# A two-layer decoder trunk on one core: the down products' add to the residual moves from VectorE into PSUM, with copies by ScalarE

## The chip, the core and the metric

The kernel runs on one core of a Trainium2 chip. The core has a matrix engine (TensorE, PE in the profile, with its weight loads as PEld), a vector engine (VectorE, DVE), a scalar engine (ScalarE, ACT), a general engine (GpSimd, POOL) and a queue that issues transfers (SyncE, SP). Each engine works through its own instructions in the order in which they stand; semaphores make one wait for another. Matrix products go to PSUM, eight banks of 128 x 512 fp32 numbers; everything else lies in SBUF. The metric is the device time of one execution in microseconds. Between two versions, a difference under 0.2% is about what a measurement can't tell from none.

## The reference

The trunk has two layers on 256 tokens of width 2048. Each layer has a token mixer with a cross-attention and then a SwiGLU feed-forward block; the residual `h` runs through all of it. The change touches the second line below, in both layers.

```
h = h + jnp.concatenate([y, xa], axis=-1) @ w_out[layer]
hn = _rmsnorm(h, norm_ffn[layer])
gate, up = jnp.split(hn @ w_gate_up[layer], 2, axis=-1)   # 2048 -> 2 x 5632
h = h + (jax.nn.silu(gate) * up) @ w_down[layer]          # 5632 -> 2048
```

## The kernel before

**Precision by parts.** Weights and left factors are fp32. Each is taken apart into a high part (a cast to fp32r) and a low part (the rest), and a product is three matmuls: high x high, high x low of the weights, low of the factor x high. So every weight tile costs a DMA into a tile `raw` (4 buffers), a cast on ACT (L207) and a subtraction on DVE (L208), both written into a tile `parts` (6 buffers). The cast's result is enough for a product's first and third matmul; the second needs the subtraction. This pair is called a split below.

**The feed-forward stage** (`ffn`) goes over 11 blocks of 512 columns (b = 0 to 10). `up_block(b)` makes gate and up in one: it goes over eight pairs of weight rows with a scheme of seven products (`project_halves`), whose sums `ps[1]` to `ps[7]` (p1 to p7 below) fill seven PSUM banks. A pair of kind S splits its weights in four pieces, a to d: a and b as loaded, c and d after DVE has combined the raw tile with itself (L350 to L352). Blocks 3 to 10 have the pairs S S O S S O S S, so they end on two S. Then ACT copies p1 out to `e` (L830), DVE adds the other sums in a row (L833, first `s<-p2`, then `e<-p6`, `s<-p7`, `e<-p5` and so on), and ACT's Silu (L835) and a product on DVE (L836) end the block. Its result is transposed on PE (L160) and split into left factors (L148, L149).

**The down products.** The 5632 rows of `w_down` are cut into six parts (`PARTS`), one block or two each. `down(i, n)` multiplies part i into the n-th 512 columns of the residual with `project`: two PSUM banks, one for each half of the tokens, and per two rows of weights one split, named 192_0, 192_2, 193_0 and so on after the raw tile. Then `add_h` adds each bank to the residual with a DVE instruction (L414). After each up block from b = 1 on, two down products are done; the last part's four stand at the end, and its adds are followed by what the next layer or the output needs.

**Order.** The code is written in program order, and a scheduler that lists the instructions ahead of the run places each on its engine's queue: by priority in program order, but as soon as its inputs and a free buffer or bank are there by the scheduler's own reckoning. Banks are given out from a pool of eight as they come free. So an edit can move instructions that it does not name. Small pieces of other work (`later`, `step`) are given out between matmuls.

Names: `f_p` are the sums of an up block, `fd` those of a down product, `h` the residual, `tp` the transposes; in this stage layer 0 has the raw tiles 84 to 215, layer 1 those from 288 to 419. The functions that the change touches, with their lines:

Of the kernel before, what the change touches and what calls it, by code (L numbers as in the profile page):

```python
# [17 lines left out]
P = 128  # L18
T = 256
NT = T // P  # L20
# [15 lines left out]
def trunk_kernel(ctx: ExitStack, tc: tile.TileContext, x, mem, norm_mix, norm_ffn, norm_mem,  # L36
                 norm_final, hgrn_w_in, hgrn_lb_logits, hgrn_onorm, gla_w_in, gla_w_gk,
                 gla_b_gk, gla_onorm, w_mem_kv, w_out, w_gate_up, w_down, c_ident, c_mask, out):
    nc = tc.nc
# [15 lines left out]
    ident = const.tile([P, P], F32, name="ident")  # L55
# [15 lines left out]
    h = const.tile([P, NT, D], F32, name="h")  # L71
# [83 lines left out]
    def transposes(srcs, name):  # L155

        ps = aux_ps(name)
        for k, src in enumerate(srcs):
            for t in range(NT):
                nc.tensor.transpose(out=ps[:, k * T + t * P:k * T + (t + 1) * P], in_=src(t), identity=ident)  # L160
        return ps

    def make_quad(quad, src, gains, same=False):

# [36 lines left out]
    def split(src, name, by=2):  # L201

        n, m = src.shape[1:]
        both = wts.tile([P, 2, 2, 512], F32R, tag="parts", name=f"parts{name}", bufs=6)
        for k in range(0, n, by):
            j = min(k + by, n)
            nc.scalar.copy(out=both[:, 0, k:j, 0:m], in_=src[:, k:j, :])  # L207
            nc.vector.tensor_tensor(out=both[:, 1, k:j, 0:m], in0=src[:, k:j, :],  # L208
                                    in1=both[:, 0, k:j, 0:m].bitcast(F32), op=ALU.subtract)
        return [(both[:, 0, k, 0:m], both[:, 1, k, 0:m]) for k in range(n)]  # L210

    def weights(w, k0, nk, c0, n):
        i, raw = new_raw()
        m = 1 if i == 0 else nk
        for j in range(0, nk, m):
            nc.sync.dma_start(out=raw[:, j:j + m, 0:n],
                              in_=w[(k0 + j) * P:(k0 + j + m) * P, c0:c0 + n].rearrange("(k p) c -> p k c", p=P))
        return [p for k in range(0, nk, 2) for p in split(raw[:, k:k + 2, 0:n], f"{i}_{k}", 1 if i == 0 else 2)]

    def project(quads, order, w, c0, n, name, parts=None, prep=None, by_tile=None):  # L220

        parts = parts or [(0, n)]
        ps = [[mm_ps(f"{name}_{i}_{t}") for t in range(NT)] for i in range(len(parts))]
        if by_tile is None:
            groups = [([qi], range(NT)) for qi in range(len(order))]
        else:
            groups = [(range(len(order)), [t]) for t in range(NT)]  # L230
        got = {}
        for qis, ts in groups:
            for qi in qis:
                q = order[qi]
                if prep:
                    prep(q)
                if qi not in got:
                    got[qi] = weights(w, 4 * q, 4, c0, n)
                for k, (hi, lo) in enumerate(got[qi]):
                    if k == 2 or (k == 0 and qi > 0):  # L240
                        step()
                    first = qi == 0 and k == 0
                    last = qi == len(order) - 1 and k == 3
                    for t in ts:
                        xh = quads[q].h[:, k, t * P:(t + 1) * P]
                        xl = quads[q].l[:, k, t * P:(t + 1) * P]
                        for i, (o, m) in enumerate(parts):
                            acc = ps[i][t][:, 0:m]
                            nc.tensor.matmul(acc, xh, hi[:, o:o + m], start=first, stop=False)  # L249
                            nc.tensor.matmul(acc, xh, lo[:, o:o + m], start=False, stop=False)  # L250
                            nc.tensor.matmul(acc, xl, hi[:, o:o + m], start=False, stop=last)  # L251
            if by_tile is not None:
                by_tile(ts[0], ps[0][ts[0]])
        return ps if len(parts) > 1 else ps[0]
# [66 lines left out]
    def project_halves(forms, kinds, w, c0, c1, name):  # L321


        left = {b: sum(TIMES[kind][b - 1] for kind in kinds) for b in range(1, 8)}
        ps = {}

        def product(b, left_factor, right):
            first = b not in ps
            if first:
                ps[b] = bank(f"{name}p{b}")  # L330
            left[b] -= 1
            (xh, xl), (hi, lo) = left_factor, right
            nc.tensor.matmul(ps[b], xh, hi, start=first, stop=False)  # L333
            nc.tensor.matmul(ps[b], xh, lo, start=False, stop=False)  # L334
            nc.tensor.matmul(ps[b], xl, hi, start=False, stop=left[b] == 0)  # L335

        for p, kind in enumerate(kinds):
            i, raw = new_raw()

            for j, c in ((slice(0, 4, 3), c0), (slice(1, 3), c1)):  # L340
                nc.sync.dma_start(out=raw[:, j, :],
                                  in_=w[2 * p * P:(2 * p + 2) * P, c:c + 512].rearrange("(k p) c -> p k c", p=P))
            x = forms[p].get
            last = p == len(PAIRS) - 1
            if kind == "S":
                tt = nc.vector.tensor_tensor
                b00, = split(raw[:, 0:1, :], f"{i}a")
                b11, b10 = split(raw[:, 2:4, :], f"{i}b")

                tt(out=raw[:, 0:2, :], in0=raw[:, 0:4:2, :], in1=raw[:, 1:2, :].broadcast_to([P, 2, 512]), op=ALU.subtract)  # L350
                tt(out=raw[:, 2, :], in0=raw[:, 2, :], in1=raw[:, 0, :], op=ALU.add)  # L351
                tt(out=raw[:, 3, :], in0=raw[:, 3, :], in1=raw[:, 2, :], op=ALU.subtract)  # L352
                t5, t7 = split(raw[:, 0:2, :], f"{i}c")
                t6, t4 = split(raw[:, 2:4, :], f"{i}d")
                todo = {1: ("x00", b00), 2: ("x01", b10), 3: ("z", b11), 4: ("x11", t4), 5: ("s", t5), 6: ("u", t6),
                        7: ("d0", t7)}
                for b in (1, 2, 6, 7, 5, 4, 3) if last else (1, 3, 2, 5, 7, 6, 4):
                    product(b, x(todo[b][0]), todo[b][1])
            else:
                b00, b01 = split(raw[:, 0:2, :], f"{i}a")  # L360
                b11, b10 = split(raw[:, 2:4, :], f"{i}b")
                todo = [[(2, "x00", b00), (5, "x10", b01), (4, "x10", b00), (3, "d0", b01)]]
                if kind == "O":
                    todo.append([(2, "x01", b10), (5, "x11", b11), (4, "x11", b10), (3, "d1", b11)])
                else:
                    nc.vector.tensor_tensor(out=raw[:, 3, :], in0=raw[:, 3, :], in1=raw[:, 2, :], op=ALU.subtract)
                    e1, = split(raw[:, 3:4, :], f"{i}c")
                    todo.append([(2, "x01", b10), (3, "x01", b11), (7, "x11", b11), (4, "x11", e1)])
                todo = [m for ms in zip(*todo) for m in ms] if last else todo[0] + todo[1]
                for b, f, right in todo:  # L370
                    product(b, x(f), right)
            step()
        return ps
# [14 lines left out]
    def h_forms(forms, n, gain, ss, name):  # L388

        for t in range(NT):  # L390
            square_sum(h[:, t, n * 512:(n + 1) * 512], ss[:, t, n:n + 1], f"{name}{n}{t}")

        def turn(p):
            forms[p] = Forms(p, f"{name}{p}")
            ps = aux_ps(f"tp_{name}{p}")
            for i, (t, k) in enumerate(((1, 0), (0, 0), (0, 1), (1, 1))):
                c = (2 * p + k) * P
                nc.tensor.transpose(out=ps[:, i * P:(i + 1) * P], in_=h[:, t, c:c + P], identity=ident)
            forms[p].put(ps, [gain[:, 2 * p + k:2 * p + k + 1] for k in range(2)])

        later(lambda: turn(2 * n), lambda: turn(2 * n + 1))
# [9 lines left out]
    def add_h(ps, c0, n):  # L411
        for t in range(NT):
            hs = h[:, t, c0:c0 + n]
            nc.vector.tensor_tensor(out=hs, in0=ps[t][:, 0:n], in1=hs, op=ALU.add)  # L414
# [402 lines left out]
    PARTS = ((0,), (1, 2), (3, 4), (5, 6), (7, 8), (9, 10))  # L817
# [4 lines left out]
    def ffn(l, forms, r, after, tail=None):  # L822
# [21 lines left out]
        def down(i, n):  # L844
            end = i == len(PARTS) - 1
            if end and n == NQ - 1 and tail:
                flush()
                project(sq, PARTS[i], w_down[l], 512 * n, 512, f"fd{l}_{i}_{n}", by_tile=tail)
                return
            ps = project(sq, PARTS[i], w_down[l], 512 * n, 512, f"fd{l}_{i}_{n}")  # L850
            add_h(ps, 512 * n, 512)
            if end:
                after(n)

        todo = []
        for b in range(DFF // 512):
# [101 lines left out]
```

## Time and profile before

| | us |
|---|---|
| median of three runs | 2323.41 |
| lowest and highest | 2322.97, 2323.65 |
| the profiled execution | 2322.12 |
| its span (first to last instruction) | 2320.3 |
| feed-forward of layer 0, its first and last matmul start | 540.9, 1244.0 |
| feed-forward of layer 1, its first and last matmul start | 1610.0, 2310.6 |

PE's granted clock is 0.998 of full speed over the span. The page of the profile gives busy time as a share of the span for each engine; such a share is a mean over stages. In this kernel the mixers (the time ahead of 540.9 and from 1244.0 to 1610.0 us) and the feed-forward stages differ: DVE is busy in 5 to 6 tenths of most slices in the first and in 9 tenths of most in the second. Rows of single instructions give the start from the span's beginning, the duration, the engine, the line, the operation, what it writes and reads, shapes, and in brackets how long the engine had been idle before it and what ended that. Matmuls overlap: a row's duration is longer than the time to the next start.

### The profile page before, as it was taken

What the parts mean: (1) busy time and instruction counts of PE and PEld (TensorE: products, weight loads), DVE (VectorE), ACT (ScalarE), POOL (GpSimd) and SP (SyncE); (2) the same over time, 40 slices, a digit from 0 to 9 for tenths busy, and PEclk for the clock granted to TensorE, in tenths of its full rate; (3) what the DMA queues carried; (4) which work ended last, traced back from release to release, by engine and by line L of the source; (5) the groups of instructions that cost most, each with busy time, mean ns of one, the idle gap of its engine ahead of it and who ended that gap; (6) DMA issues with size and microseconds to landing.
All of it is one profiled execution on the core that took longest, in us unless ns stands there. A gap on an engine that the chain in (4) does not pass through costs nothing.

```text
span 2320.3 us, 28901 instructions
## 1 busy us (share of the span) xinstructions
PE 2297.6 (99%) x11034; PEld 1934.7 (83%) x11034; DVE 1887.7 (81%) x2262; ACT 1261.2 (54%) x1643; POOL 22.2 (1%) x39
## 2 busy tenths in 40 slices
PE   9999999999999999999999999999999999999998
PEld 7888888888887888888889999988887888888886
DVE  5566565668999999999985665567999999999995
ACT  7543534455555555555555654455555555555563
POOL 0000000000000000000000000000000000000000
PEclk9999999999999999999999999999999999999999
DMA  8554545455556556566565445555555556656563
GB/s 316 192 172 162 164 150 176 145 182 176 186 188 212 200 188 205 189 209 208 183 226 167 150 150 167 161 199 164 178 203 198 201 187 210 202 189 210 200 217 127
DMA packets 229211, 435.51 MB, mean 188 GB/s; under 512 B 10028, under 2 KB 38992, under 8 KB 228816
## 3 DMA queue, kind: packets, MB, share of 16 engines
q1 hardware_dynamic: 227776, 429.40, 55.5%
q10 hardware_dynamic: 1296, 4.26, 0.5%
q8 instruction: 86, 1.41, 0.2%
q14 instruction: 53, 0.43, 0.1%
HBM read 430.48 MB, written 3.15 MB: 187 GB/s over the span
## 4 chain that ended last, share of the span: by engine, by line
PE 63%; DVE 25%; issue 6%; ACT 4%; DMA 0%; ACTq 0%; DVEq 0%; POOLq 0%; SPq 0%
PE f_p L334 5%; PE f_p L335 5%; PE f_p L333 4%; DVE raw L350 4%; DVE parts L208 4%; PE fd L250 3%; PE fd L249 3%; PE fd L251 3%; PE wo L251 3%; PE wo L249 3%; PE wo L250 3%; DVE raw L351 2%; DVE raw L352 2%; PE hgate L249 1%; PE gv L249 1%
## 5 line engine op out<-in xcount | busy, mean ns | idle before, releaser
L208 DVE TENSOR_TENSOR parts<-raw,parts 128x1024 fp32r<-128x1024 f32 (+3 forms) x490 | 557.7, 1147 | 289.1 <-ACT parts L207 288.2
L207 ACT CAST parts<-raw 128x1024 fp32r<-128x1024 f32 (+3 forms) x490 | 476.8, 991 | 424.6 <-PE wo L251 64.4
L350 DVE TENSOR_TENSOR raw<-raw 128x1024 f32<-128x1024 f32 x118 | 143.6, 1217 | 0.2
L351 DVE TENSOR_TENSOR raw<-raw 128x512 f32<-128x512 f32 x118 | 81.6, 692 | 3.9
L352 DVE TENSOR_TENSOR raw<-raw 128x512 f32<-128x512 f32 x118 | 81.6, 692 | 3.8
L414 DVE TENSOR_TENSOR h<-fd,h 128x512 f32<-128x512 f32 x94 | 61.9, 684 | 6.2 <-PE fd L251 6.1
L833 DVE TENSOR_TENSOR e<-f_p,e 128x512 f32<-128x512 f32 x66 | 44.9, 680 | 0.0
L835 ACT ACTIVATE s<-s,rf_r 128x512 f32<-128x512 f32 x44 | 31.8, 722 | 6.9 <-DVE s L833 6.9
L836 DVE SCALAR_TENSOR_TENSOR s<-e,rf_r,s 128x512 f32<-128x512 f32 x44 | 32.3, 742 | 0.0
L562 DVE COPY_PREDICATED sch<-mask,slh 96x512 f32<-96x512 uint8 (+3 forms) x15 | 10.8, 721 | 25.1 <-PE slh L578 25.1
L833 DVE TENSOR_TENSOR s<-f_p,e 128x512 f32<-128x512 f32 x44 | 29.5, 682 | 0.0
L578 PEld LDWEIGHTS slh<-Q,K 128*96 128x96 f32 (+3 forms) x240 | 25.4, 176 | 1.4
L249 PE MATMUL wo<-parts,y_3h 128*128 128x512 f32 x64 | 25.9, 405 | 0.0
L249 PE MATMUL wo<-parts,y_0h 128*128 128x512 f32 x64 | 25.7, 402 | 0.0
L250 PE MATMUL fd<-parts,s_3h 128*128 128x512 f32 x64 | 25.4, 396 | 0.0
L249 PE MATMUL fd<-parts,s_0h 128*128 128x512 f32 x64 | 25.3, 396 | 0.0
L249 PE MATMUL fd<-parts,s_2h 128*128 128x512 f32 x64 | 25.3, 396 | 0.0
L249 PE MATMUL fd<-parts,s_6h 128*128 128x512 f32 x64 | 25.3, 396 | 0.0
L249 PE MATMUL fd<-parts,s_4h 128*128 128x512 f32 x64 | 25.3, 396 | 0.0
L250 PE MATMUL fd<-parts,s_5h 128*128 128x512 f32 x64 | 25.3, 396 | 0.0
L249 PE MATMUL fd<-parts,s_8h 128*128 128x512 f32 x64 | 25.3, 396 | 0.0
L250 PE MATMUL fd<-parts,s_0h 128*128 128x512 f32 x64 | 25.3, 396 | 0.0
(5486 smaller groups left out, 7396.4 us busy)
## 6 DMA issues: line engine op xcount, KB each, us to landing
raw<-in_w_gate_up_dram SPq DMA_DIRECT2D x352, 512.0 KB, 4.0
raw<-in_w_down_dram SPq DMA_DIRECT2D x88, 1024.0 KB, 5.0
raw<-in_hgrn_w_in_dram SPq DMA_DIRECT2D x52, 1024.0 KB, 5.0
raw<-in_gla_w_in_dram SPq DMA_DIRECT2D x48, 768.0 KB, 4.3
raw<-in_w_out_dram SPq DMA_DIRECT2D x32, 1024.0 KB, 4.9
raw<-in_w_mem_kv_dram SPq DMA_DIRECT2D x15, 1024.0 KB, 8.2
raw<-in_gla_w_in_dram SPq DMA_DIRECT2D x8, 528.0 KB, 3.7
mtok<-in_mem_dram SPq DMA_DIRECT2D x4, 512.0 KB
```

Of the source, the lines that this page charges most:

```text
L207: nc.scalar.copy(out=both[:, 0, k:j, 0:m], in_=src[:, k:j, :])
L208: nc.vector.tensor_tensor(out=both[:, 1, k:j, 0:m], in0=src[:, k:j, :], in1=both[:, 0, k:j, 0:m].bitcast(F32), op=ALU.subtract)
L249: nc.tensor.matmul(acc, xh, hi[:, o:o + m], start=first, stop=False)
L250: nc.tensor.matmul(acc, xh, lo[:, o:o + m], start=False, stop=False)
L251: nc.tensor.matmul(acc, xl, hi[:, o:o + m], start=False, stop=last)
L333: nc.tensor.matmul(ps[b], xh, hi, start=first, stop=False)
L334: nc.tensor.matmul(ps[b], xh, lo, start=False, stop=False)
L335: nc.tensor.matmul(ps[b], xl, hi, start=False, stop=left[b] == 0)
L350: tt(out=raw[:, 0:2, :], in0=raw[:, 0:4:2, :], in1=raw[:, 1:2, :].broadcast_to([P, 2, 512]), op=ALU.subtract)
L351: tt(out=raw[:, 2, :], in0=raw[:, 2, :], in1=raw[:, 0, :], op=ALU.add)
L352: tt(out=raw[:, 3, :], in0=raw[:, 3, :], in1=raw[:, 2, :], op=ALU.subtract)
L833: nc.vector.tensor_tensor(out=out, in0=ps[p], in1=q, op=ALU.add)
```

## The change

A down product of parts 0 to 4 no longer starts on an empty bank. Before its first matmul, ACT copies the residual's 512 columns into the two banks (L244 of the changed kernel, "put there"), and the matmuls all accumulate. The sum of residual and product is then copied back to the residual by ACT (L232, "taken back"), and the add on DVE falls away: 80 of 94 instructions of L414. The copy back is not given out behind its product. It is held in a list (`held`) and given out later by `give_back`: in the next down product behind the casts of its first weights, or in the next up block, with a pair that isn't S, or with an S pair from the second on, behind the first casts of that pair. The two banks stay taken until then. The last part's products (part 5) are as before.

That a bank accumulates onto what ACT put there depends on marks that matmuls leave in it, so the transposes are written in another way too (`turns`): of the transposes into one bank only the first starts afresh, and the bank is left marked as written all over. Their number and sizes are the same.

```diff
+    def turns(ps, srcs):
+        for i, src in enumerate(srcs):
+            nc.tensor.matmul(ps[:, i * P:(i + 1) * P], src, ident, start=i == 0, stop=i == len(srcs) - 1,
+                             is_transpose=True, skip_group_check=True)
...
+    held = []
+    def give_back():
+        while held:
+            hs, ps = held.pop(0)
+            for t in range(NT):
+                nc.scalar.copy(out=hs[:, t, :], in_=ps[t])
...
+        if onto:
+            for t in range(NT):
+                nc.scalar.copy(out=ps[0][t], in_=onto(t))
...
                     got[qi] = weights(w, 4 * q, 4, c0, n)
+                    give_back()
...
-                    first = qi == 0 and k == 0
+                    first = qi == 0 and k == 0 and not onto
...
+            if kind != "S":
+                give_back()
             if kind == "S":
                 b00, = split(raw[:, 0:1, :], f"{i}a")
                 b11, b10 = split(raw[:, 2:4, :], f"{i}b")
+                if p > 0:
+                    give_back()
...
-            ps = project(sq, PARTS[i], w_down[l], 512 * n, 512, f"fd{l}_{i}_{n}")
-            add_h(ps, 512 * n, 512)
             if end:
+                ps = project(sq, PARTS[i], w_down[l], 512 * n, 512, f"fd{l}_{i}_{n}")
+                add_h(ps, 512 * n, 512)
                 after(n)
+                return
+            hs = h[:, :, 512 * n:512 * n + 512]
+            ps = project(sq, PARTS[i], w_down[l], 512 * n, 512, f"fd{l}_{i}_{n}", onto=lambda t: hs[:, t, :])
+            held.append((hs, ps))
```

The scheduler then places much of the stage anew. Two places recur in each block. The first is the end of an up block, here block 9 of layer 0 with its last raw tile 191; 192_0 is the first split of the down product behind it. DVE before:

```order
L208 TENSOR_TENSOR parts191c_8261<-raw191_8249,parts191c_8261 128x1024
L833 TENSOR_TENSOR s0_9_8289<-f0_9_p2_8007,e0_9_8288 128x512
L208 TENSOR_TENSOR parts191d_8264<-raw191_8249,parts191d_8264 128x1024
L208 TENSOR_TENSOR parts192_0_8306<-raw192_8304,parts192_0_8306 128x1024
L833 TENSOR_TENSOR e0_9_8288<-f0_9_p6_8019,e0_9_8288 128x512
L208 TENSOR_TENSOR parts192_2_8309<-raw192_8304,parts192_2_8309 128x1024
```

The same place on DVE now, and what follows up to the split of 193_0:

```order
L213 TENSOR_TENSOR parts191c_8293<-raw191_8281,parts191c_8293 128x1024
L855 TENSOR_TENSOR s0_9_8321<-f0_9_p2_8037,e0_9_8320 128x512
L213 TENSOR_TENSOR parts191d_8296<-raw191_8281,parts191d_8296 128x1024
L855 TENSOR_TENSOR e0_9_8320<-f0_9_p6_8049,e0_9_8320 128x512
L213 TENSOR_TENSOR parts192_0_8340<-raw192_8338,parts192_0_8340 128x1024
L855 TENSOR_TENSOR s0_9_8321<-f0_9_p7_8045,e0_9_8320 128x512
L213 TENSOR_TENSOR parts192_2_8343<-raw192_8338,parts192_2_8343 128x1024
```

The add of p6 has moved ahead of the split of 192_0, and each later split of the down weights by one add; the split of 193_0, which stood behind `s<-p7`, now stands behind `e<-p5` (twice), `e<-p3`, `s<-p4` and a product. It is so at the ends of blocks 4 to 10 in both layers. On PE, p6's and p4's last matmuls, which stood behind the first two of the down product, now stand ahead of them. On ACT, at the same place, before:

```order
L207 CAST parts191c_8261<-raw191_8249 128x1024
L830 COPY e0_9_8288<-f0_9_p1_7999 128x512
L207 CAST parts191d_8264<-raw191_8249 128x1024
L207 CAST parts192_0_8306<-raw192_8304 128x1024
L835 ACTIVATE s0_9_8289<-s0_9_8289,rf0_r_3976 128x512
```

And ACT now:

```order
L212 CAST parts191c_8293<-raw191_8281 128x1024
L852 COPY e0_9_8320<-f0_9_p1_8029 128x512
L212 CAST parts191d_8296<-raw191_8281 128x1024
L244 COPY fd0_4_0_0_1_8335<-h_87 128x512
L857 ACTIVATE s0_9_8321<-s0_9_8321,rf0_r_3976 128x512
L212 CAST parts192_0_8340<-raw192_8338 128x1024
```

The second of the two copies into PSUM stands there (it gets the bank that the copy of p1 frees), and the cast of 192_0 has moved behind it and behind the Silu.

The second place is the start of the next up block, here the first two pairs of block 9 (raw tiles 184 and 185). DVE before:

```order
L208 TENSOR_TENSOR parts184d_7996<-raw184_7981,parts184d_7996 128x1024
L414 TENSOR_TENSOR h_87<-fd0_3_3_0_0_7913,h_87 128x512
L414 TENSOR_TENSOR h_87<-fd0_3_3_0_1_7914,h_87 128x512
L208 TENSOR_TENSOR parts185a_8030<-raw185_8027,parts185a_8030 128x512
L208 TENSOR_TENSOR parts185b_8033<-raw185_8027,parts185b_8033 128x1024
L350 TENSOR_TENSOR raw185_8027<-raw185_8027 128x1024
L351 TENSOR_TENSOR raw185_8027<-raw185_8027 128x512
L352 TENSOR_TENSOR raw185_8027<-raw185_8027 128x512
L208 TENSOR_TENSOR parts185c_8039<-raw185_8027,parts185c_8039 128x1024
L208 TENSOR_TENSOR parts185d_8042<-raw185_8027,parts185d_8042 128x1024
```

DVE now:

```order
L213 TENSOR_TENSOR parts184d_8026<-raw184_8011,parts184d_8026 128x1024
L213 TENSOR_TENSOR parts185a_8060<-raw185_8057,parts185a_8060 128x512
L374 TENSOR_TENSOR raw185_8057<-raw185_8057 128x1024
L213 TENSOR_TENSOR parts185b_8063<-raw185_8057,parts185b_8063 128x1024
L375 TENSOR_TENSOR raw185_8057<-raw185_8057 128x512
L213 TENSOR_TENSOR parts185c_8071<-raw185_8057,parts185c_8071 128x1024
L376 TENSOR_TENSOR raw185_8057<-raw185_8057 128x512
L213 TENSOR_TENSOR parts185d_8074<-raw185_8057,parts185d_8074 128x1024
```

The two adds are gone, and the combinations of the raw tile stand between the splits. On ACT the copies back stand there now:

```order
L212 CAST parts185a_8060<-raw185_8057 128x512
L232 COPY h_87<-fd0_3_3_0_0_7941 128x512
L212 CAST parts185b_8063<-raw185_8057 128x1024
L232 COPY h_87<-fd0_3_3_0_1_7942 128x512
L212 CAST parts185c_8071<-raw185_8057 128x1024
L244 COPY fd0_4_0_0_0_8334<-h_87 128x512
L212 CAST parts185d_8074<-raw185_8057 128x1024
```

Before, these four casts stood behind each other. The first pair of copies back of each period stands one pair earlier, between the casts of 184a and 184b. The first copy into PSUM for the next down product is given out here, most of an up block ahead of that product, since its bank is free.

More of the change, by code (lines that the diff above doesn't have):

```diff
@@ L157, in transposes @@
         ps = aux_ps(name)
-        for k, src in enumerate(srcs):
-            for t in range(NT):
-                nc.tensor.transpose(out=ps[:, k * T + t * P:k * T + (t + 1) * P], in_=src(t), identity=ident)
-        return ps
+        turns(ps, [src(t) for src in srcs for t in range(NT)])
+        return ps
+    def turns(ps, srcs):
+        for i, src in enumerate(srcs):
+            nc.tensor.matmul(ps[:, i * P:(i + 1) * P], src, ident, start=i == 0, stop=i == len(srcs) - 1,
+                             is_transpose=True, skip_group_check=True)
     def make_quad(quad, src, gains, same=False):
@@ L218, in weights, with project @@
         return [p for k in range(0, nk, 2) for p in split(raw[:, k:k + 2, 0:n], f"{i}_{k}", 1 if i == 0 else 2)]
-    def project(quads, order, w, c0, n, name, parts=None, prep=None, by_tile=None):
+    held = []
[4 more added lines that the diff above has]
+                nc.scalar.copy(out=hs[:, t, :], in_=ps[t])
+    def project(quads, order, w, c0, n, name, parts=None, prep=None, by_tile=None, onto=None):
         parts = parts or [(0, n)]
         ps = [[mm_ps(f"{name}_{i}_{t}") for t in range(NT)] for i in range(len(parts))]
+        if onto:
+            for t in range(NT):
+                nc.scalar.copy(out=ps[0][t], in_=onto(t))
         if by_tile is None:
@@ L248, in project @@
                             acc = ps[i][t][:, 0:m]
-                            nc.tensor.matmul(acc, xh, hi[:, o:o + m], start=first, stop=False)
-                            nc.tensor.matmul(acc, xh, lo[:, o:o + m], start=False, stop=False)
-                            nc.tensor.matmul(acc, xl, hi[:, o:o + m], start=False, stop=last)
+                            free = dict(skip_group_check=True) if onto else {}
+                            nc.tensor.matmul(acc, xh, hi[:, o:o + m], start=first, stop=False, **free)
+                            nc.tensor.matmul(acc, xh, lo[:, o:o + m], start=False, stop=False, **free)
+                            nc.tensor.matmul(acc, xl, hi[:, o:o + m], start=False, stop=last, **free)
             if by_tile is not None:
@@ L395, in turn @@
             ps = aux_ps(f"tp_{name}{p}")
-            for i, (t, k) in enumerate(((1, 0), (0, 0), (0, 1), (1, 1))):
-                c = (2 * p + k) * P
-                nc.tensor.transpose(out=ps[:, i * P:(i + 1) * P], in_=h[:, t, c:c + P], identity=ident)
+            turns(ps, [h[:, t, (2 * p + k) * P:(2 * p + k + 1) * P] for t, k in ((1, 0), (0, 0), (0, 1), (1, 1))])
             forms[p].put(ps, [gain[:, 2 * p + k:2 * p + k + 1] for k in range(2)])
```

## The prediction

> **What bounds the kernel now.** I read the page first: shares of the engines, then one steady stretch of the feed-forward stage by itself, then its waits, then single instructions in order of time on VectorE (DVE), TensorE (PE) and ScalarE (ACT) around the two places where the change moves work.
>
> ```profile
> PE 2297.6 (99%) x11034; PEld 1934.7 (83%) x11034; DVE 1887.7 (81%) x2262; ACT 1261.2 (54%) x1643; POOL 22.2 (1%) x39
> L414 DVE TENSOR_TENSOR h<-fd,h 128x512 f32<-128x512 f32 x94 | 61.9, 684 | 6.2 <-PE fd L251 6.1
> ```
>
> The shares are means over stages. The next row is one period, from the last weights of block 8 to those of block 9 (two down products and an up block), in the window view: its start and end, its length, then busy time of PE, PEld, DVE, ACT, POOL.
>
> ```profile
> 1045.22:1108.38 63.16, 62.93 (x279) 51.17 (x280) 62.44 (x70) 36.09 (x42) 0.00 (x0) 1.00 0.60 200
> ```
>
> DVE is busy 62.44 of 63.16 us, and PE's matmuls leave almost nothing either: two engines are level, and ACT has 27 us free. Which one ends last is told by PE's waits in this stage of layer 0 (waiter, released by, total, times, longest). Layer 1 has the same rows under other tile numbers.
>
> ```profile
> PE f_p L333 <- ACT parts113d L207: 0.7, 1, 0.7
> PE f_p L333 <- ACT parts116d L207: 0.5, 1, 0.5
> ...
> PE f_p L333 <- ACT parts191d L207: 0.2, 1, 0.2
> ```
>
> PE waits at the end of each block, for the last two pieces of weights (c and d); block 3 has two waits more. Behind those casts stands DVE, as the chain of waits shows at block 9's end (start, us on the chain, what).
>
> ```profile
> 1110.12 1.22 DVE parts191d L208
> 1111.33 1.14 DVE parts L208
> 1112.47 0.60 DVE e L833
> ```
>
> So the block end is DVE's, instruction after instruction. What it does there, and what PE does beside it:
>
> ```profile
> 1109.52 0.68 DVE L833 TENSOR_TENSOR s<-f_p,e 128x512 f32<-128x512 f32 x1
> 1110.12 1.22 DVE L208 TENSOR_TENSOR parts191d<-raw,parts191d 128x1024 fp32r<-128x1024 f32 x1
> 1111.25 1.22 DVE L208 TENSOR_TENSOR parts<-raw,parts 128x1024 fp32r<-128x1024 f32 x1
> 1112.38 0.68 DVE L833 TENSOR_TENSOR e<-f_p,e 128x512 f32<-128x512 f32 x1
> 1112.99 1.21 DVE L208 TENSOR_TENSOR parts<-raw,parts 128x1024 fp32r<-128x1024 f32 x1
> 1118.25 0.74 DVE L836 SCALAR_TENSOR_TENSOR s<-e,rf_r,s 128x512 f32<-128x512 f32 x1
> 1118.91 1.22 DVE L208 TENSOR_TENSOR parts<-raw,parts 128x1024 fp32r<-128x1024 f32 x1
> ```
>
> ```profile
> 1107.87 0.39 PE L333 MATMUL f_p<-parts191b,hf_7h 128*128 128x512 f32 x1
> 1108.22 0.73 PE L333 MATMUL f_p<-parts191c,hf_7h 128*128 128x512 f32 x2
> 1109.03 0.40 PE L335 MATMUL f_p<-parts191b,hf_7l 128*128 128x512 f32 x1
> 1109.66 0.50 PE L333 MATMUL f_p<-parts191d,hf_7h 128*128 128x512 f32 x1 [0.23 <-ACT parts191d L207]
> 1111.61 0.39 PE L334 MATMUL f_p<-parts191d,hf_7h 128*128 128x512 f32 x1
> 1111.83 0.39 PE L335 MATMUL f_p<-parts191d,hf_7l 128*128 128x512 f32 x1
> 1112.52 0.50 PE L250 MATMUL fd<-parts,s_7h 128*128 128x512 f32 x1
> ```
>
> Read off: a DVE split occupies 1.13 us (1111.25 to 1112.38) and its result is there after 1.22; a 512-wide DVE operation occupies 0.60; a matmul follows the last after 0.23 and ends 0.39 after its start. PE starts L250 0.05 after the split it needs (1111.25 + 1.22 = 1112.47).
>
> **The change, part by part.** *Off DVE:* 80 of the 94 adds of L414, four per block at 0.60, so 2.4 us of a 63.16 us period, 48 us in all. *Onto ACT:* 160 copies. A copy out of PSUM has its row below (0.58, the next instruction 0.47 later); one into PSUM has none, and I put it between that and the 512-wide cast's 0.61 (both rows stand with the block start). That is 8 x 0.48 = 3.8 us a block on an engine with 27 free. *Transposes* with other accumulate flags: the same number of the same instructions, nothing. SyncE's and GpSimd's rows are in the old order, so no load is issued in another place.
>
> *The block end (costs).* The order of DVE now puts `e<-p6` ahead of the first split of the down weights (192_0). `e<-p6` reads a PSUM product that PE can finish only when the split of 191d is there: DVE now waits for PE, which has just waited for DVE, and PE's first low-part product (L250) stands behind both. Step by step from the rows: split of 191d ends 1110.12 + 1.22 = 1111.34; p6's L334 at 1111.39, L335 at 1111.62, ended 1112.01; `e<-p6` starts 1112.06; the split of 192_0 0.60 later, 1112.66, ends 1113.88; L250 starts 1113.93 in place of 1112.52: **+1.41**. PE is out of work from about 1112.75 (two products of p4 and two of fd behind p6). Bounds: 0.60 if DVE finds p6 ready and only `e<-p6` moves in between, 1.6 if both hand-overs between engines take 0.1 more.
>
> *The next split (costs).* 193_0 also falls back, behind four combinations. DVE from 1112.66: 1.13 + 0.60 + 1.13 + 4 x 0.60 + 0.66 (1118.25 to 1118.91) + 1.22, so 1119.80. PE from 1113.93 has 24 products of 0.227 and two transposes, 1119.4 to 1119.85 if a transpose costs from nothing to a product. A second wait of 0 to 0.45: I take the middle, **+0.25**.
>
> *The block start (gains).* The second pair of adds stood here (columns as before):
>
> ```profile
> 1071.24 1.37 DVE L414 TENSOR_TENSOR h<-fd,h 128x512 f32<-128x512 f32 x2
> 1072.53 0.68 DVE L208 TENSOR_TENSOR parts185a<-raw,parts185a 128x512 fp32r<-128x512 f32 x1
> 1073.13 1.22 DVE L208 TENSOR_TENSOR parts185b<-raw,parts185b 128x1024 fp32r<-128x1024 f32 x1
> ...
> 1076.24 0.69 DVE L352 TENSOR_TENSOR raw<-raw 128x512 f32<-128x512 f32 x1
> 1076.85 1.22 DVE L208 TENSOR_TENSOR parts185c<-raw,parts185c 128x1024 fp32r<-128x1024 f32 x1
> 1078.13 1.23 DVE L208 TENSOR_TENSOR parts185d<-raw,parts185d 128x1024 fp32r<-128x1024 f32 x1
> ```
>
> ```profile
> 1061.04 1.05 ACT L207 CAST parts184b<-raw 128x1024 fp32r<-128x1024 f32 x1 [1.07 <-PE fd L251]
> 1069.95 0.61 ACT L207 CAST parts185a<-raw 128x512 fp32r<-128x512 f32 x1
> 1071.96 1.06 ACT L207 CAST parts185b<-raw 128x1024 fp32r<-128x1024 f32 x1 [1.40 <-issue]
> 1077.04 1.05 ACT L207 CAST parts185d<-raw 128x1024 fp32r<-128x1024 f32 x1 [0.40 <-DVE raw L352]
> 1108.08 0.58 ACT L830 COPY e<-f_p 128x512 f32<-128x512 f32 x1
> 1108.55 1.05 ACT L207 CAST parts191d<-raw 128x1024 fp32r<-128x1024 f32 x1
> 1110.45 0.72 ACT L835 ACTIVATE s<-s,rf_r 128x512 f32<-128x512 f32 x1
> 1111.08 4.83 ACT L207 CAST parts<-raw 128x1024 fp32r<-128x1024 f32 x5
> ```
>
> ACT casts 185b only at 1071.96, after an idle 1.40: the six buffers of split weights are full, and PE must read one empty (the row of 185b names no releaser, that of 184b names PE). DVE can't be further ahead than that, with adds or without. New order from there: split of 185b at 1073.07 (cast's end + 0.05), L351 1074.20, 185c 1074.80, L352 1075.93, its end 1076.62, cast of 185d 0.11 later (as 1077.04 follows 1076.93) and 1.05 long, split of 185d at 1077.83 in place of 1078.13: **-0.30**. Of 2.4 us taken off DVE, 0.3 arrive; the rest is DVE idle before the casts of 185b and 185d. From there to 191d DVE's order is the old one and without a gap, so PE's waits there stay but for this. Bounds: nothing, or 0.5 (all of PE's wait at the block end, below).
>
> *Block 3 (gains).* Its 0.7 and 0.5 come from a lead that block 2 did not build. With four adds less before it I count the first as gone, the second (16 us later) not: **-0.7** a layer; bounds 0 and -1.2.
>
> *ACT's place (nothing, while covered).* Ahead of the cast of 192_0 now stand a copy into PSUM and the Silu, which needs DVE's `s<-f_p` (ends 1110.20): Silu 1110.31 to 1110.94, cast ends 1111.99, and PE needs it about 1112.3. Cover 0.3; without it PE waits that much longer, but it then waits for the split anyway. The copies back stand before casts of 184b and 185b; PE reads 184b first after 1072.
>
> *Sum.* DVE's order is changed in this way at the ends of blocks 4 to 10 of both layers: 14 x (1.41 + 0.25 - 0.30) = 19.0; block 3 twice, -1.4; together **+17.6** on the profiled execution's 2322.12 (span 2320.3): 2339.7. The median of the runs, 2323.41, stands 1.3 above that execution, so **2341**. With all bounds low, 14 x (0.60 - 0.50) - 2.4, -1; with all high, 14 x 2.05, +29.
>
> **Rivals.**
> *Faster: DVE was the bound, and what is taken off it shows.* For it: 62.44 of 63.16, and DVE behind every wait of PE. The price is what PE loses there: 1107.87 to 1108.22 and 1109.03 to 1109.66 exceed 0.23 by 0.12 and 0.40, so 0.52 at 16 block ends, 8.3, and 1.2 twice in block 3: -10.7, **2313**. Against it: buffers cap the lead at 1071.96, and the first split moves behind `e<-p6`. It decides if DVE reaches 191c 0.5 us earlier and L250 does not wait. In the Trainium skill, Perfetto Trace Analysis, Identifying the Most-Contended Engine, occupancy tells the bound for VectorE and that engine is to be relieved first, TensorE being judged by its weight loads; here DVE's 62.44 stands against PEld's 51.17, so by that rule this rival holds. The trace agrees on who is fullest, not that less work for it moves its next due instruction.
> *Same: the loop DVE-PE-DVE is short.* If p6 is done when DVE arrives, 14 x (0.60 - 0.30) - 1.4 = +2.8, **2326**. Against it: p6 can't end before 1112.01, DVE is free at 1111.25.
> *Slower still: ACT becomes late.* If the two copies back (2 x 0.48), which wait for the first down product's end, push the cast of 184b onto PE in 20 blocks, +19 on top: **2360**. It decides when the cast is late by more than its lead, 1061.04 to about 1072: 11 us speak against it. The Trainium skill, ScalarE: Activation LUTs, Rules for kernel authors, sends adds to VectorE and not ScalarE; here two copies of 0.58 do take longer than one add of 0.68, but by ACT's 36.09 of 63.16 they find room.
>
> **How the numbers follow.** Forecast 0.77, faster 0.10, same 0.06, ACT late 0.07. A difference under 0.2% (4.6 us) can't be told from none here. The range 2328 to 2356 holds the forecast with its upper bound (2352) and part of the ACT case, and leaves out the faster one and most of the same one. Slower 0.83, same 0.07, faster 0.10.
>
> **What will show it.** In the changed profile: 14 adds left, 160 copies near 0.5 to 0.6 us; DVE idle about 0.8 before `e<-p6`, released by PE; PE waiting about 1.2 for the first down weights' split at 14 block ends; periods of 64.5 in place of 63.16, DVE near 60 busy in them, ACT near 40. I am wrong if periods are shorter than 63.2, if L250's counterpart starts right behind its neighbours, or if PE waits for a copy or for the casts behind the copies back.

## The result, and the profile after

The changed kernel takes 2341.91 us in the median (2341.46 to 2342.41), the kernel before 2323.19 beside it: a ratio of 1.0081, 95% interval 1.0067 to 1.0095. It is 0.8% slower, by 18.7 us. The profiled execution stands at 2341.61, 19.5 above that of before.

The page of the changed kernel: shares of the engines, then groups of instructions (busy us, mean ns of one, idle time of the engine ahead of them and what ended it). L232 is the copy back, L244 the copy into PSUM, L855 what was L833.

```profile
PE 2304.6 (98%) x11034; PEld 1933.0 (83%) x11034; DVE 1842.7 (79%) x2182; ACT 1345.0 (57%) x1803; POOL 22.2 (1%) x39
...
L232 ACT COPY h<-fd 128x512 f32<-128x512 f32 x80 | 46.7, 587 | 44.0 <-PE fd L271 42.3
L855 DVE TENSOR_TENSOR e<-f_p,e 128x512 f32<-128x512 f32 x66 | 45.1, 684 | 11.5 <-PE f_p L355 11.5
L244 ACT COPY fd<-h 128x512 f32<-128x512 f32 x80 | 45.4, 583 | 0.0
```

DVE is busy 45 us less than before and ACT 84 more; a copy takes as long into PSUM (583 ns) as out of it (587). The waits of both feed-forward stages hold two rows that before has none of:

```profile
PE fd L270 <- DVE parts L213: 13.9, 14, 1.0
...
DVE e L855 <- PE f_p L355: 11.5, 14, 0.8
```

Fourteen times PE waits for DVE's split of the first down weights, and fourteen times DVE waits for PE's product p6. The chain of waits at the end of block 9 shows that these are one loop (start, us on the chain, what):

```profile
1119.16 0.24 PE f_p L355
1119.40 0.03 issue
1119.42 0.03 DVE e L855
1119.46 0.57 issue
1120.03 1.23 DVE parts L213
1121.26 0.04 issue
1121.30 0.51 PE fd L270
```

The chain runs from PE to DVE and back to PE; before, it ran through DVE alone here. The same place on DVE and PE in order of time, with the matmuls on both sides of the second wait:

```profile
1117.39 1.22 DVE L213 TENSOR_TENSOR parts191d<-raw,parts191d 128x1024 fp32r<-128x1024 f32 x1
1119.42 0.69 DVE L855 TENSOR_TENSOR e<-f_p,e 128x512 f32<-128x512 f32 x1 [0.82 <-PE f_p L355]
1120.03 1.22 DVE L213 TENSOR_TENSOR parts<-raw,parts 128x1024 fp32r<-128x1024 f32 x1
...
1125.95 1.22 DVE L213 TENSOR_TENSOR parts<-raw,parts 128x1024 fp32r<-128x1024 f32 x1
```

```profile
1118.66 0.50 PE L354 MATMUL f_p<-parts191d,hf_7h 128*128 128x512 f32 x1
1118.99 0.39 PE L355 MATMUL f_p<-parts191d,hf_7l 128*128 128x512 f32 x1
...
1119.69 0.63 PE L269 MATMUL fd<-parts,s_7h 128*128 128x512 f32 x2
1121.30 0.51 PE L270 MATMUL fd<-parts,s_7h 128*128 128x512 f32 x1 [0.98 <-DVE parts L213]
1121.64 0.39 PE L271 MATMUL fd<-parts,s_7l 128*128 128x512 f32 x1
...
1126.77 0.48 PE L269 MATMUL fd<-parts,s_8h 128*128 128x512 f32 x1
1127.22 0.50 PE L270 MATMUL fd<-parts,s_8h 128*128 128x512 f32 x1
```

The row at 1119.69 holds two matmuls; the second starts 0.23 behind the first, at 1119.92, so L270 follows it after 1.38 instead of 0.23: PE loses 1.15. The last DVE row is the split of 193_0. It ends at 1127.17, L270 starts 0.05 later, and PE loses 0.45 - 0.23 = 0.22 there. The window view gives the period, from the split of 179c to that of 191c as in the prediction:

```profile
1051.02:1115.65 64.63, 63.41 (x279) 51.06 (x280) 60.22 (x66) 40.30 (x50) 0.00 (x0) 1.00 0.58 196
```

64.63 instead of 63.16, with DVE busy 60.2 and ACT 40.3. Where DVE's free time went at the block's start, the prediction's second place:

```profile
1080.54 1.23 DVE L213 TENSOR_TENSOR parts185b<-raw,parts185b 128x1024 fp32r<-128x1024 f32 x1 [1.16 <-ACT parts185b L212]
1081.80 0.69 DVE L375 TENSOR_TENSOR raw<-raw 128x512 f32<-128x512 f32 x1
...
1085.40 1.23 DVE L213 TENSOR_TENSOR parts185d<-raw,parts185d 128x1024 fp32r<-128x1024 f32 x1 [1.18 <-ACT parts185d L212]
```

DVE stands idle for 1.16 + 1.18 = 2.34 us until two casts are there, which is about what the four adds of 0.60 had taken.

### The profile page after: what moved, and what is told of

The parts are those of the page before. It is cut to its first block, busy times and chain, and to the rows that moved or that the text cites. A ratio compares the mean times of both kernels' runs of the same rounds, so it can differ in the third digit from the quotient of the medians.

```text
span 2339.8 us, 28935 instructions
## 1 busy us (share of the span) xinstructions
PE 2304.6 (98%) x11034; PEld 1933.0 (83%) x11034; DVE 1842.7 (79%) x2182; ACT 1345.0 (57%) x1803; POOL 22.2 (1%) x39
## 3 DMA queue, kind: packets, MB, share of 16 engines
q8 instruction: 86, 1.41, 0.2%
## 4 chain that ended last, share of the span: by engine, by line
PE 70%; DVE 19%; issue 6%; ACT 4%; DMA 0%; SPq 0%; ACTq 0%; DVEq 0%; POOLq 0%
PE fd L270 7%; PE fd L271 7%; PE fd L269 6%; PE f_p L354 4%; PE f_p L355 4%; PE f_p L353 3%; DVE raw L374 3%; PE wo L271 2%; PE wo L269 2%; PE wo L270 2%; DVE raw L375 2%; DVE raw L376 2%; PE hgate L269 1%; PE gv L269 1%; PE ggate L269 1%
## 5 line engine op out<-in xcount | busy, mean ns | idle before, releaser
L232 ACT COPY h<-fd 128x512 f32<-128x512 f32 x80 | 46.7, 587 | 44.0 <-PE fd L271 42.3
L855 DVE TENSOR_TENSOR e<-f_p,e 128x512 f32<-128x512 f32 x66 | 45.1, 684 | 11.5 <-PE f_p L355 11.5
L244 ACT COPY fd<-h 128x512 f32<-128x512 f32 x80 | 45.4, 583 | 0.0
L855 DVE TENSOR_TENSOR s<-f_p,e 128x512 f32<-128x512 f32 x44 | 29.6, 683 | 0.0
L270 PE MATMUL fd<-parts,s_3h 128*128 128x512 f32 x64 | 25.4, 396 | 4.0 <-DVE parts L213 4.0
L270 PE MATMUL fd<-parts,s_5h 128*128 128x512 f32 x64 | 25.4, 396 | 4.0 <-DVE parts L213 4.0
L270 PE MATMUL fd<-parts,s_7h 128*128 128x512 f32 x64 | 25.4, 396 | 4.0 <-DVE parts L213 4.0
L270 PE MATMUL fd<-parts,s_1h 128*128 128x512 f32 x64 | 25.2, 394 | 2.0 <-DVE parts L213 2.0
L270 PE MATMUL fd<-parts,s_6h 128*128 128x512 f32 x64 | 25.4, 397 | 0.0
L270 PE MATMUL fd<-parts,s_8h 128*128 128x512 f32 x64 | 25.4, 397 | 0.0
L270 PE MATMUL fd<-parts,s_4h 128*128 128x512 f32 x64 | 25.4, 397 | 0.0
```

The source lines that it names most:

```text
L855: nc.vector.tensor_tensor(out=out, in0=ps[p], in1=q, op=ALU.add)
```

## The experiments

The theory under test has two halves. (1) The loss is an order: a copy into PSUM stands ahead of the first down weights' cast, that cast falls behind the Silu, and DVE's split falls behind `e<-p6`. (2) What is taken off DVE brings little, since its lead is capped where the cast of 185b waits. The rivals are the copies' own time, and DVE as the bound.

### Both copies into PSUM later

```diff
-        if onto:
-            for t in range(NT):
-                nc.scalar.copy(out=ps[0][t], in_=onto(t))
...
                     give_back()
+                    if onto and qi == 0:
+                        for t in range(NT):
+                            nc.scalar.copy(out=ps[0][t], in_=onto(t))
```

> The changed kernel with one thing moved: both copies of the residual into PSUM are given out behind the casts of the down product's first weights instead of ahead of them. All 160 copies stay on ScalarE, the 80 adds stay off VectorE, and the order of VectorE at the ends of blocks 4 to 10 is the old one again (first split of the down weights ahead of e<-p6). Theory (the loss is the order at the block end, made by the place of the copy): the 14 waits of about 1 us of PE for the first down weights are gone, periods are 63.2 or a little less, and the time is 2318 to 2325 us; relief of VectorE still brings only block 3's 0.7 a layer and some tenths a block. Rival one (the copies' own time on ScalarE or in the banks costs): the time stays within 4 us of 2341.9. Rival two (VectorE was the bound and its relief shows once the order is repaired): 2313 or less.

Measured: 2321.34 us, against 2322.87 of before beside it; ratio 0.9993, interval 0.9984 to 1.0002. That is 20.6 below the changed kernel, with the same number of copies. ACT at the end of block 9, and the period:

```profile
1109.09 1.05 ACT L212 CAST parts191d<-raw 128x1024 fp32r<-128x1024 f32 x1
1110.05 1.04 ACT L212 CAST parts<-raw 128x1024 fp32r<-128x1024 f32 x1
1110.99 0.72 ACT L857 ACTIVATE s<-s,rf_r 128x512 f32<-128x512 f32 x1
1111.62 1.03 ACT L212 CAST parts<-raw 128x1024 fp32r<-128x1024 f32 x1
1112.56 0.58 ACT L257 COPY fd<-h 128x512 f32<-128x512 f32 x1
```

```profile
1045.78:1108.92 63.14, 62.91 (x279) 51.10 (x280) 60.13 (x66) 40.16 (x50) 0.00 (x0) 1.00 0.59 200
```

The cast of 192_0 stands behind that of 191d again, the copy two casts later, and none of the 14 waits is left. The changed kernel has these rows instead:

```profile
1115.82 1.05 ACT L212 CAST parts191d<-raw 128x1024 fp32r<-128x1024 f32 x1
1116.78 0.58 ACT L244 COPY fd<-h 128x512 f32<-128x512 f32 x1
1117.51 0.72 ACT L857 ACTIVATE s<-s,rf_r 128x512 f32<-128x512 f32 x1
1118.13 5.78 ACT L212 CAST parts<-raw 128x1024 fp32r<-128x1024 f32 x6
```

With the order repaired the period is that of before, 63.14 for 63.16, though DVE has 2.3 us less to do in it. The order makes the loss, and relieving DVE brings nothing in this period. From first matmul to first matmul, two stretches of each layer do get shorter: from block 3 to block 4 it is 64.51 and 64.54 for 64.86 and 64.88, and from block 5 to block 6 63.16 and 63.15 for 63.45 and 63.43.

Two orders change together at the block end, ScalarE's and DVE's, and no run changes one alone. The rows allow an estimate. The cast of 192_0 starts at 1118.13 and takes 1.05, and DVE is free from 1118.5 on. Had `e<-p6` not stood ahead of it, the split of 192_0 could have started at about 1119.2 instead of 1120.03, and PE would have lost about 0.3 of its 1.15. So some 0.8 is DVE's order, and some 0.3 is the cast's place behind the Silu.

### No copy into PSUM at all

```diff
-        if onto:
-            for t in range(NT):
-                nc.scalar.copy(out=ps[0][t], in_=onto(t))
...
-                    first = qi == 0 and k == 0 and not onto
+                    first = qi == 0 and k == 0
```

> The changed kernel without the copies into PSUM; a down product starts on an empty bank, and the copy back stays. It leaves the residual out of the sum, so its result lacks it. VectorE's order at the block end is the old one. Theory (order): as with the copies given out late, 2317 to 2324 us. Rival (the copy back costs the time): near 2341. Rival (copies into PSUM cost by their own ScalarE time): this is faster than the kernel that gives them out late by more than 3 us.

Measured: 2321.76 us, ratio 0.9994 (0.9985 to 1.0004). Leaving the 80 copies out gains nothing over giving them out later; their own time costs nothing that can be measured.

### The copies back cut to one column

```diff
-            for t in range(NT):
-                nc.scalar.copy(out=hs[:, t, :], in_=ps[t])
+            nc.scalar.copy(out=hs[:, 0, 0:1], in_=ps[0][:, 0:1])
+            nc.scalar.copy(out=hs[:, 1, 0:1], in_=ps[1][:, 0:1])
```

> The changed kernel with each copy back cut from 128 x 512 to 128 x 1 elements: it leaves the writing back to the residual out, but for one column. The copies into PSUM are where the change put them, and so is the order at the block end. Theory (order): the loss stays, 2337 to 2343 us, with 14 waits of PE of about 1 us. Rival (the copies back, 80 x 0.58 us, cost it): 2323 to 2331.

Measured: 2340.96 us, ratio 1.0078 (1.0064 to 1.0092). The loss stays, and so does its row in the waits of PE:

```profile
PE fd L270 <- DVE parts L213: 13.9, 14, 1.0
```

Cutting the copies back brings 1 us at most.

### A copy on ScalarE at that place, in the kernel before

```diff
+            if lead:
+                spare = work.tile([P, 512], BF16, tag="junk", name=f"spare{l}_{i}_{n}")
+                nc.scalar.copy(out=spare, in_=lead.pop())
             add_h(ps, 512 * n, 512)
```

Here `lead` holds the bank of p1 from block 4 on, and the scheduler puts the copy at the block's end.

> The kernel before, with one more ScalarE copy of 128 x 512 out of PSUM at the place where the change has the second copy into PSUM: behind the cast of the block's last piece of weights, ahead of the cast of the first down weights, at the ends of blocks 4 to 10. It writes a spare tile that nobody reads. VectorE's order is the old one. Theory (the order, not ScalarE's time, costs): 2322 to 2326 us; the first down weights' cast ends about 0.5 later, which the lead over VectorE covers. Rival (ScalarE's time at the block end is on the path): 14 x 0.5, so 2330 us or more.

Measured: 2322.86 us, ratio 1.0000 (0.9991 to 1.0009). ACT at the end of block 9:

```profile
1109.25 1.05 ACT L207 CAST parts191d<-raw 128x1024 fp32r<-128x1024 f32 x1
1110.20 0.58 ACT L854 CAST spare<-f_p 128x512 bf16<-128x512 f32 x1
1110.68 1.05 ACT L207 CAST parts<-raw 128x1024 fp32r<-128x1024 f32 x1
1111.63 0.72 ACT L837 ACTIVATE s<-s,rf_r 128x512 f32<-128x512 f32 x1
```

A copy of the same 0.58, out of PSUM and not into it, stands ahead of the cast of 192_0, which does not fall behind the Silu here, and DVE's order is the old one: it costs nothing. So it is not the 0.58 us on ScalarE. What differs between this kernel and the changed one at this place is the order.

### Half a dose: late in layer 1 only

```diff
-        if onto:
+        if onto and name[2] == "0":
...
+                    if onto and qi == 0 and name[2] == "1":
+                        for t in range(NT):
+                            nc.scalar.copy(out=ps[0][t], in_=onto(t))
```

> The changed kernel with the copies into PSUM moved behind the first weights' casts in layer 1 alone; layer 0 is as the change has it, so the order at the block end is the new one at 7 places and the old one at the other 7. Theory (each place costs the same by itself): the changed kernel and the one with all copies late are 20.6 us apart over 14 places, 1.47 each; 2321.3 + 7 x 1.47 = 2331.6, so 2330 to 2333, with 7 waits of 1.0 us of PE for the first down weights in layer 0 and none in layer 1. Rival (the loss builds up over the places, or one early delay carries it): clearly off that middle, under 2327 or over 2337.

Measured: 2331.84 us, ratio 1.0036 (1.0023 to 1.0049), and in the waits of PE half of the row:

```profile
PE fd L273 <- DVE parts L213: 6.9, 7, 1.0
```

L273 is L270 of that kernel. The seven places of layer 0 cost 10.5 us more than the kernel with all copies late, and the seven of layer 1 would cost 10.1 more: each place costs by itself, 1.4 to 1.5 us.

### The adds off VectorE, and nothing else

```diff
-            add_h(ps, 512 * n, 512)
             if end:
+                add_h(ps, 512 * n, 512)
                 after(n)
+            else:
+                for t in range(NT):
+                    nc.vector.tensor_copy(h[:, t, 512 * n:512 * n + 1], ps[t][:, 0:1])
```

> The kernel before with its 80 adds of 128 x 512 on VectorE cut to copies of 128 x 1: it leaves the down products' add to the residual out, so its result lacks them. No copy is put on ScalarE and nothing into PSUM, and the order at the block end is the old one. It measures what taking the adds off VectorE brings by itself, some 42 us of its work. Theory (VectorE's lead is capped by the buffers of split weights): idle time of VectorE before the next pair's casts takes the place of the adds, and only block 3 and some tenths a block arrive: 2317 to 2322 us. Rival (VectorE is the bound and the copies on ScalarE ate the gain): 2313 or less.

Measured: 2318.41 us, ratio 0.9979 (0.9970 to 0.9988): DVE is busy 40.6 us less (1847.1), and 4.7 of it arrive. None comes from the periods; the window view gives 63.18:

```profile
1044.07:1107.25 63.18, 62.95 (x279) 51.16 (x280) 60.38 (x70) 36.06 (x42) 0.00 (x0) 1.00 0.60 200
```

```profile
1072.13 1.23 DVE L208 TENSOR_TENSOR parts185b<-raw,parts185b 128x1024 fp32r<-128x1024 f32 x1 [0.84 <-ACT parts185b L207]
...
1077.01 1.23 DVE L208 TENSOR_TENSOR parts185d<-raw,parts185d 128x1024 fp32r<-128x1024 f32 x1 [1.19 <-ACT parts185d L207]
```

DVE idles 0.84 + 1.19 there instead, as these rows at the start of block 9 show. The gain is in block 3 above all: from its first matmul to that of block 4 the layers take 63.20 and 63.18, and 64.86 and 64.88 before, so 3.4 of the 4.7.

### The same work taken off DVE at two places

Both kernels are the kernel before, with one combination of the raw tile cut from 128 x 512 to 128 x 1 in blocks 4 to 10; p is 6 in the one (late) and 0 in the other (early).

```diff
-                tt(out=raw[:, 3, :], in0=raw[:, 3, :], in1=raw[:, 2, :], op=ALU.subtract)
+                m = 1 if p == 6 and int(name.split("_")[1]) >= 4 else 512
+                tt(out=raw[:, 3, 0:m], in0=raw[:, 3, 0:m], in1=raw[:, 2, 0:m], op=ALU.subtract)
```

> The kernel before, with 0.6 us of VectorE work less in each of blocks 4 to 10, 14 in all: the third combination of the raw tile (L352) of the last pair but one (raw tile 190 in block 9) is cut from 128 x 512 to 128 x 1, which leaves that combination out but for one column. The order of VectorE, ScalarE and the loads is the old one. The place lies behind the cast that waits for a buffer and ahead of the block end. Theory (VectorE's work counts only between that cast and the block end): nearly all of PE's wait for the last pieces, about 0.5 a block, goes: 14 x 0.4 to 0.55, so 2315 to 2318 us. Rival (nothing on VectorE counts, PE is the floor at 63.16 a period): 2322 to 2324.

> The same cut, one column of 512 left, in the first pair of the same 14 blocks (raw tile 184 in block 9), in place of the last but one; it leaves that combination out. The place lies ahead of the cast that waits for a buffer, where the adds stood. Theory (VectorE runs against the buffers there): VectorE idles 0.5 longer before the cast of the next pair and nothing arrives: 2321.5 to 2324 us. Rival (VectorE is the bound, any work taken off it counts): as in the late place, 2318 or less.

Measured: late 2318.68 us, ratio 0.9980 (0.9971 to 0.9989); early 2323.30, ratio 1.0000 (0.9992 to 1.0009). Behind the cut, DVE of the late kernel and of the early one:

```profile
1099.96 0.16 DVE L353 TENSOR_TENSOR raw<-raw 128x1 f32<-128x1 f32 x1
1100.39 1.23 DVE L208 TENSOR_TENSOR parts190c<-raw,parts190c 128x1024 fp32r<-128x1024 f32 x1 [0.28 <-ACT parts190c L207]
1101.54 1.22 DVE L208 TENSOR_TENSOR parts190d<-raw,parts190d 128x1024 fp32r<-128x1024 f32 x1
1102.67 0.69 DVE L208 TENSOR_TENSOR parts191a<-raw,parts191a 128x512 fp32r<-128x512 f32 x1
```

```profile
1069.36 0.16 DVE L353 TENSOR_TENSOR raw<-raw 128x1 f32<-128x1 f32 x1
1069.79 1.23 DVE L208 TENSOR_TENSOR parts184c<-raw,parts184c 128x1024 fp32r<-128x1024 f32 x1 [0.27 <-ACT parts184c L207]
...
1072.43 1.37 DVE L415 TENSOR_TENSOR h<-fd,h 128x512 f32<-128x512 f32 x2 [0.27 <-PE fd L251]
```

The cut combination occupies DVE for 0.43 - 0.28 = 0.15 instead of 0.60, so 0.45 is taken off, and 0.28 of it is lost to a cast. The split of 190d follows that of 190c after 1.15, in the kernel before after 1.28. From the combination to the split of 191a it is 2.71 instead of 3.03 (1101.03 to 1104.06 before), so 0.32 arrives: 14 x 0.32 = 4.5 us, as measured (2323.14 - 2318.68). I had expected 0.4 to 0.55 a block, since I had not reckoned with that cast. The early cut loses 0.27 to a cast and 0.27 to PE, and nothing arrives. The same instruction is worth 4.5 us at one place and nothing at the other. The starts of three DVE splits say why (us between them, block 9):

| | 179d to 185d | 185d to 191d | both |
|---|---|---|---|
| before | 31.17 | 31.99 | 63.16 |
| copies into PSUM late | 31.16 | 31.98 | 63.14 |
| adds off DVE | 31.21 | 31.98 | 63.19 |
| early cut | 31.20 | 32.00 | 63.20 |
| late cut | 31.18 | 31.68 | 62.86 |
| changed kernel | 32.65 | 31.99 | 64.64 |

The second stretch is DVE's own work, instruction behind instruction. The first doesn't shrink with DVE's work: it ends behind the cast of 185b, for which ACT waits; in the kernel without adds its row names the releaser:

```profile
1071.04 1.05 ACT L207 CAST parts185b<-raw 128x1024 fp32r<-128x1024 f32 x1 [2.10 <-PE fd L251]
```

ACT has been idle for 2.10 us until PE was through with a product of the weights ahead. Of the kernels in the table, the stretch is longer in the changed one alone, where PE itself waits in it. So the period is a loop: PE lets a cast go, DVE works 32 us from there, and PE waits for the last piece. That the number of `parts` buffers sets the cast's time is read from the code and from these waits; it was not varied.

### Only the transposes in the new form

```diff
-            for t in range(NT):
-                nc.tensor.transpose(out=ps[:, k * T + t * P:k * T + (t + 1) * P], in_=src(t), identity=ident)
+            pass
+        turns(ps, [src(t) for src in srcs for t in range(NT)])
...
```

> The kernel before with only the transposes written as in the change (of those into one bank only the first starts afresh, the same number of instructions of the same size). Theory: no difference, 2322 to 2324 us. Rival (accumulating transposes are slower, or the order shifts): 2326 or more.

Measured: 2323.16 us, ratio 0.9999 (0.9990 to 1.0008). Nothing.

### One step further

The kernel with both copies late gets one more pair of kind S, in block 2. Such a pair only pays where DVE and ACT have room for it:

```diff
-    KINDS = ("SHOSHOSO", "SHOSSOSO", "SHOSSOSO", "SSOSSOSS")
+    KINDS = ('SHOSHOSO', 'SHOSSOSO', 'SSOSSOSO', 'SSOSSOSS')
```

> The kernel with both copies into PSUM given out late, and one step more: in block 2 the first two pairs of weight rows are of kind S instead of S and H, which takes three matmuls out of each layer and adds VectorE and ScalarE work there, where the lead is larger. Theory: 1 to 4 us below 2321.3, so 2317 to 2320.5. Rival (ScalarE and VectorE become late in block 2): 2321 or more.

Measured: 2318.81 us, ratio 0.9981 (0.9972 to 0.9990). It is the fastest kernel here that leaves no work out, 4.3 us or 0.19% under the kernel before: the interval doesn't reach 1, but the gain is not above the 0.2% that the prediction took as its bound. Whether the same pair would gain in the kernel before was not run.

## Why the prediction was right, step by step

The forecast was 2341 in the median and +17.6 on the profiled execution; measured were 2341.91 and +19.5. The sign, the place and the mechanism are as forecast, and the runs show them. Two terms of the sum were wrong, by 0.26 and 0.30 a block, and nearly cancelled, so that the number came this close is partly luck.

**The block end.** Every sign came: 14 places, DVE idle 0.82 before `e<-p6` (forecast about 0.8), PE losing 1.15 (about 1.2), L270 0.05 behind the end of its split. But the term of +1.41 was the wrong quantity. It is the shift of one matmul against DVE's split of 191d (measured: 3.91 in place of 2.40, +1.51), and part of that is matmuls that PE does anyway. A period pays PE's idle time only, 1.15, which the prediction had beside it (out of work from 1112.75 to 1113.93, so 1.18) and did not put into the sum.

**The next split.** The forecast was +0.25, between 0 and 0.45, and 0.22 was measured.

**The block start.** Forecast -0.30, measured nothing: 31.16 in place of 31.17 in the kernel with the old order, and no shorter without copies. The step that failed put the split of 185b at 0.05 behind an unmoved cast and the rest of DVE's rows at their old distances. In the kernel with the old order the cast came 25.20 behind the split of 179d, in place of 25.00, and the combination behind the split of 185b followed after 1.26 in place of the 1.13 assumed. These two took the 0.30 back. The mechanism, a capped lead, was right, and stronger than put.

With 1.15 + 0.22 and no gain at the block start the sum is 1.37 of the 1.47 by which a period grew. The rows of PE account for the other 0.10, though no run tests it. A matmul that starts about 0.05 behind what it waits for is followed after 0.33 or 0.34 instead of 0.23. The changed kernel has four of these at this place (1116.92, 1118.66, 1121.30 and 1127.22), the kernel before two (1109.66 and 1112.52), which makes 0.2. Of that, 0.09 goes off again, since the first matmul behind the transposes loses it before as well (1119.82 to 1120.14).

**Block 3.** Forecast -0.7 a layer; the stretch from its first matmul to that of block 4 is 0.52 shorter in both (64.34 for 64.86, 64.36 for 64.88). The first wait went, the second stayed at 0.6. In all, 14 x 1.47 - 2 x 0.52 = 19.5, the difference between the profiled executions. That this fits to the tenth is chance too. From block 5 to block 6 the period grew by 1.18 and 1.25 only. And block 3 of layer 0 starts 0.90 later in this execution (691.69 for 690.79), where two kernels with the code of before up to there, the early and the late cut, start it at 691.79 and 691.27: so much differs between executions.

**The copies and the transposes.** Hidden, as forecast: 583 and 587 ns, and no measurable cost by the kernels without copies into PSUM and with one-column copies back; the transposes cost nothing.

**The rivals.** *DVE as the bound* fell: the kernel with only the adds gone gained 4.7 and not 10.7, none of it in the periods. The Trainium skill, Perfetto Trace Analysis, Identifying the Most-Contended Engine, would relieve the fullest engine first; the trace does not agree here: DVE was the fullest beside PE (62.44 of 63.16), and the same operation cut in each block brought 4.5 us in one place and nothing in another. *ACT late* fell: the cast of 184b never held PE, and cutting the copies back gained at most 1 us. *A short loop* fell with the 0.82.

## What to carry to other kernels

Where two engines hand work to each other, look at the order at the hand-over before the busy shares: a copy of 0.6 us that was free by itself cost 1.5 at each of 14 places by where it stood, since with it there one split fell behind an instruction that waits for the other engine. Cut the period at the places where an engine waits for a buffer, and count work taken off only if it stands between that wait and the one that ends the stretch. And add up the idle time of the engine that sets the pace, not the shift of single instructions.

## What was not expected of the hardware

ScalarE writes 128 x 512 fp32 numbers into PSUM as fast as it reads them out of it (583 and 587 ns over 80 copies each), while the prediction had allowed up to 0.61. A VectorE operation of 128 x 1 still occupies the trace for 0.16 us, against 0.69 for 128 x 512. Behind a wait, the first matmul is followed by the next after 0.34 us and not after 0.23 (1121.30 to 1121.64 in the changed kernel); the prediction's 0.23 a matmul left that out. The matmuls at 1118.66 in the changed kernel and at 1112.52 before show it too, though their own rows name no wait; there it was the weight load ahead that had waited for DVE's split, by 0.28 and 0.27. Why the next one comes later stays open.
